# Second-layer memory keys and values projected between the sparse attention's queries and its items, and kept in DRAM

## The chip, the core and the metric

The kernel runs on one core of a Trainium2 chip. The metric is the device time of one execution in microseconds (us); lower is better. PE is TensorE (matrix products), DVE is VectorE, ACT is ScalarE, POOL is GpSimd, and SP is SyncE, whose in-order queue issues nearly all DMAs here.

## What is computed

Two decoder layers over 512 tokens of width 1024. Layer 0 mixes tokens with latent attention, layer 1 with a sparse attention: an indexer scores keys, the best 128 keys of each query stay, and 16 heads in 4 groups attend to them. After the mixer, each layer attends to 256 memory tokens with 4 heads, and then applies an FFN. The part that the change touches is the memory attention of the second layer:

```
def memory_cross_attention(x, mem, w_q, w_kv, w_o):
    q = (x @ w_q).reshape(b, s, XA_HEADS, XA_HEAD_DIM)
    kv = (mem @ w_kv).reshape(b, m, 2, XA_HEADS, XA_HEAD_DIM)
    k, v = kv[:, :, 0], kv[:, :, 1]
    logits = jnp.einsum('bshd,bmhd->bhsm', q, k).astype(jnp.float32) * (XA_HEAD_DIM ** -0.5)
    p = jax.nn.softmax(logits, axis=-1).astype(v.dtype)
    o = jnp.einsum('bhsm,bmhd->bshd', p, v)
    return o.reshape(b, s, D_MODEL) @ w_o
```

`k` and `v` depend on the memory tokens alone, not on the layer's own state. The top-k selection is `lax.top_k(score, topk)` for each block of 128 queries.

## The kernel before

**Number format.** Every fp32 operand is split into a high and a low half (`split`, L94: ACT casts the high half, L95; DVE or, where `eng` is given, POOL subtracts to get the low half, L96). A product is three matmuls (`mm3`, L115 to L118). A weight chunk (`chunk`, L103) is a 512 KB load into a tile `raw` (3 buffers), split into `wh` and `wl` (5 buffers each). PSUM has banks under the tags "a" and "b"; working tiles are `t` (the small ones of 512 columns, or the large ones of 4x512, of which there are 9).

**Order.** Each engine runs its instructions in a fixed order, which a scheduler settles when the program is built; it follows the order in which the code is written unless something later could go earlier. An instruction that waits holds up all that stands behind it on its engine, and a DMA on SP that waits for its buffer holds up the DMAs behind it.

**The stretch around the change.** In the second layer, after the indexer, DVE runs the top-k rounds (`topk`, L948): 16 rounds for each of three query blocks, each a MAX8 (L953) and a MATCH_REPLACE8 (L954) over 256, 384 or 512 columns, and after a block's last round one TENSOR_SCALAR (L958) that turns the scores into a mask. The rounds are dealt out in the code: 2 before each of 2 key projections, 5 (`NTK`) before each of the 8 query projections `w_q`, 1 (`NTI`) after each item. A query projection is 24 matmuls of 512 columns; its result leaves PSUM through `stack_q_pool` (L891 to L897): one copy and two casts on ACT, two subtractions of 64x512 on POOL.

Then come 16 items (4 query blocks by 4 groups), each with scores (`dsa_scores`, L996; 12 matmuls), a softmax whose row maximum is taken on DVE (L399) and whose exponential is on ACT (L405), transposes (L1020, L1022) and the product with the values (L1032, L1033). The bias tile of each item is loaded from `scr` on SP. The output projection `dsa_o` follows with a LayerNorm for each of four token tiles (L295 to L334).

**Memory attention** (`cross`, L703). The keys and values of head 0 are projected just before it (`xa_kv`, L684: 96 matmuls of 256 columns; the weight halves by ACT and DVE). For each head `hd` the code writes scores, then the query projection of head `hd+1` (48 matmuls of 512 columns), then keys and values of head `hd+1`, then `pv`: 8 transposes (L735), two splits and 12 matmuls. The memory tokens themselves (`load_mem`, L672) are two `raw` tiles, loaded on SP right behind the last `w_q` chunk and split at the start of the cross stage.

Of the kernel before, what the change touches and what calls it, by code (L numbers as in the profile page):

```python
# [11 lines left out]
F32 = mybir.dt.float32  # L12
FR = mybir.dt.float32r
I32 = mybir.dt.int32
AF = mybir.ActivationFunctionType
ALU = mybir.AluOpType
# [4 lines left out]
P = 128  # L21
# [3 lines left out]
NK = D // P  # L25
# [41 lines left out]
def tile_hybrid_mla_dsa_deepnorm_block(ctx: ExitStack, tc: tile.TileContext, A: dict, out: bass.AP):  # L67
# [79 lines left out]
    scr = dp.tile([5, 16, P, GW], F32, name="scr")  # L147
    vscr = dp.tile([16, GW], F32, name="vscr")
    flag = cp.tile([1, 1], I32, name="flag")
    ones = cp.tile([P, 1], F32, name="ones")  # L150
# [520 lines left out]

    def load_mem():  # L672
        m = []
        for c in range(2):
            raw = wp.tile([P, 4, 256], F32, tag="raw", name=nm("raw"), bufs=3)
            nc.sync.dma_start(raw, A["memT"][c])
            for i in range(2):
                h, l = t2(FR, (P, 2, 256)), t2(FR, (P, 2, 256))
                split(h, l, raw[:, 2 * i:2 * i + 2])
                m += [(h[:, 0], l[:, 0]), (h[:, 1], l[:, 1])]  # L680
        return m

    def xa_kv(i, hd, m):
        pk = bank("a", (P, 2, 256))  # L684
        for dt in range(2):
            wh, wl = chunk(A["xa_k"][i, 2 * hd + dt], (P, NK, P))
            for k in range(NK):
                mm3(pk[:, dt], (wh[:, k], wl[:, k]), m[k], k == 0, k == NK - 1)
        Kt = (t2(FR, (P, 2, 256)), t2(FR, (P, 2, 256)))
        split(Kt[0], Kt[1], pk)  # L690
        ws = [chunk(A["xa_v"][i, hd, c], (P, 4, 256)) for c in range(2)]
        pv = bank("a", (P, 2, 256))
# [6 lines left out]
        split(Vt[0], Vt[1], pv)  # L699
        return Kt, Vt  # L700

    def cross(i, XT, m, kv0):
        OT = []  # L703
        kvs = {0: kv0}

# [43 lines left out]
        for hd in range(4):  # L749
            Ss = scores(hd, Q)  # L750
            if hd < 3:
                Q = q_proj(hd + 1)
                kvs[hd + 1] = xa_kv(i, hd + 1, m)
            pv(hd, Ss)
# [120 lines left out]
    out_proj(lambda k: OTs[k], lambda n, c: A["mla_o"][n, c], 4, norm, True)  # L875
    kv0 = xa_kv(0, 0, mem)
    OT = cross(0, norm.XT, mem, kv0)
    norm = Norm(load_ln(0, 1))
# [6 lines left out]
    def stack_q(ps, QA, QB):  # L885
# [3 lines left out]
        nc.vector.tensor_tensor(QB[0:64], ps[64:128], QB[64:128].bitcast(F32), op=ALU.subtract)  # L889

    def stack_q_pool(ps, QA, QB):  # L891
        f = t2()
        nc.scalar.copy(f, ps)
        nc.scalar.copy(QA[0:64], ps[0:64])
        nc.scalar.copy(QB[64:128], ps[64:128])
        nc.gpsimd.tensor_tensor(QA[64:128], f[0:64], QA[0:64].bitcast(F32), op=ALU.subtract)
        nc.gpsimd.tensor_tensor(QB[0:64], f[64:128], QB[64:128].bitcast(F32), op=ALU.subtract)  # L897

# [62 lines left out]
    todo = [(qt, [i]) for qt in range(1, NT) for i in range(TOPK // 8)]  # L961
    NTK, NTI = 5, 1
    KA, KB = [], []
# [16 lines left out]
    for j in range(8):  # L980
# [7 lines left out]
        else:  # L988
            qa, qb = t2(FR), t2(FR)
        stack_q_pool(pq, qa, qb)  # L990
        Q += [qa, qb]

    OTd = [(t2(FR), t2(FR)) for _ in range(NK)]
# [70 lines left out]
    for i in range(16):  # L1064
        a = 1 if i < LA else 0
        if i != LA:
            run_s(i + 1 + a)
            run_t(i + a)
        dsa_pv(*items[i], *PT.pop(i))
        for _ in range(NTI):  # L1070
            if todo:
                topk(*todo.pop(0))

    load_x(xsp)
    mem = load_mem()
    norm = Norm(load_ln(1, 0))
    out_proj(lambda k: OTd[k], lambda n, c: A["dsa_o"][n, c], 4, norm, True)
    kv0 = xa_kv(1, 0, mem)
    OT = cross(1, norm.XT, mem, kv0)
    norm = Norm(load_ln(1, 1))  # L1080
# [85 lines left out]
```

## Time and profile before

| what | value |
|---|---|
| median of 3 runs (lowest to highest) | 1563.23 us (1559.45 to 1563.29) |
| time of the profiled execution | 1561.3 us |
| span of the profiled execution | 1559.5 us |
| PE busy | 1513.7 us, 97% of the span |
| DVE busy | 998.4 us, 64% |
| ACT busy | 659.1 us, 42% |
| POOL busy | 306.8 us, 20% |
| mean granted PE clock | 0.994 of full speed |

Outside the span lie 1.8 us of the profiled execution. Starts in the rows below are microseconds from the start of the span. A busy PE is not PE at its peak; a stretch in which PE is idle, or its clock is low, is where time can be won.

### The profile page before, as it was taken

The page shows a single profiled execution, that of the slowest core. Times are in us where ns is not written, and L with a number is a line of the kernel's source. Part 1 is how long each engine was busy: PE and PEld are TensorE (multiplying, and loading weights), DVE is VectorE, ACT ScalarE, POOL GpSimd, SP SyncE. Part 2 cuts the span into 40 slices and gives each one's busy share as a digit, 9 for nine tenths or more (in the row PEclk, how much of TensorE's full clock was granted, in tenths as well). Part 3 has the DMA queues.
Part 4 walks back from the last instruction along what each step waited for, and adds up shares of the span by engine and source line. Part 5 has one row for each costly group of instructions (what it writes and reads, how often), then busy time and mean ns, then how long its engine had stood idle before and what let it go on. Part 6 is the DMA issues. An engine that isn't in the chain of part 4 may idle for free.

```text
span 1559.5 us, 20796 instructions
## 1 busy us (share of the span) xinstructions
PE 1513.7 (97%) x7948; PEld 1290.8 (83%) x7948; DVE 998.4 (64%) x1706; ACT 659.1 (42%) x1182; POOL 306.8 (20%) x303
## 2 busy tenths in 40 slices
PE   8999999999999999999999789999999999999997
PEld 7788778988888888888788678889888888888886
DVE  5887868454746565654668968785448466556545
ACT  4676753343233333332246489434332333333230
POOL 1322101000132331400125522010001323324002
PEclk9999999999999999999999899999999999999999
DMA  6234323322323232223241236243223132322221
GB/s 219 71 103 115 131 87 122 124 93 95 122 96 107 79 120 90 100 88 110 80 149 68 88 122 236 72 143 111 95 95 134 70 122 72 118 95 95 95 95 54
DMA packets 51320, 166.79 MB, mean 107 GB/s; under 512 B 5300, under 2 KB 11748, under 8 KB 49172
## 3 DMA queue, kind: packets, MB, share of 16 engines
q1 hardware_dynamic: 50788, 164.41, 30.8%
q8 instruction: 62, 1.02, 0.3%
q10 hardware_dynamic: 432, 1.05, 0.2%
q14 instruction: 38, 0.31, 0.1%
HBM read 161.20 MB, written 9.47 MB: 109 GB/s over the span
## 4 chain that ended last, share of the span: by engine, by line
PE 78%; DMA 8%; DVE 7%; ACT 4%; issue 1%; POOL 1%; SPq 0%; POOLq 0%; ACTq 0%; DVEq 0%
PE ps L118 24%; PE ps L116 24%; PE ps L117 24%; DMA scr<-vscr 4%; DVE t L96 2%; DVE wl L96 1%; ACT wh L95 1%; DMA raw<-in_mla_o_dram 1%; ACT t L95 1%; ACT t L405 1%; PE ps L324 1%; DVE t L954 1%; POOL sm L267 1%; PE ps L1022 1%; DVE m L953 1%
## 5 line engine op out<-in xcount | busy, mean ns | idle before, releaser
L116 PE MATMUL ps<-t,wh 128*128 128x512 f32 (+1 forms) x1264 | 459.1, 363 | 3.5 <-DVE t L96 3.4
L117 PE MATMUL ps<-t,wh 128*128 128x512 f32 (+1 forms) x1264 | 458.2, 362 | 0.9 <-DVE t L96 0.9
L118 PE MATMUL ps<-t,wl 128*128 128x512 f32 (+1 forms) x1264 | 458.1, 362 | 0.0
L95 ACT CAST wh<-raw 128x1024 fp32r<-128x1024 f32 (+2 forms) x218 | 227.4, 1044 | 470.5 <-PE ps L117 163.3
L96 DVE TENSOR_TENSOR wl<-raw,wh 128x1024 fp32r<-128x1024 f32 (+2 forms) x202 | 260.9, 1293 | 227.7 <-ACT wh L95 225.9
L116 PE MATMUL ps<-wh,t 128*128 128x512 f32 (+2 forms) x838 | 304.9, 364 | 3.8 <-DVE t L96 1.5
L118 PE MATMUL ps<-wh,t 128*128 128x512 f32 (+2 forms) x838 | 303.1, 362 | 1.0 <-DVE t L96 1.0
L117 PE MATMUL ps<-wl,t 128*128 128x512 f32 (+2 forms) x838 | 302.0, 360 | 0.0
L116 PEld LDWEIGHTS ps<-t,wh 128*128 128x128 f32 x1264 | 238.6, 189 | 41.6 <-DVE t L96 5.2
L117 PEld LDWEIGHTS ps<-t,wh 128*128 128x128 f32 x1264 | 238.6, 189 | 37.9 <-DVE t L96 1.4
L118 PEld LDWEIGHTS ps<-t,wl 128*128 128x128 f32 x1264 | 238.6, 189 | 36.7
L116 PEld LDWEIGHTS ps<-wh,t 128*128 128x128 f32 x838 | 158.8, 189 | 27.5 <-ACT t L95 1.8
L118 PEld LDWEIGHTS ps<-wh,t 128*128 128x128 f32 x838 | 158.8, 190 | 24.7 <-DVE t L96 1.4
L117 PEld LDWEIGHTS ps<-wl,t 128*128 128x128 f32 x838 | 158.9, 190 | 23.0
L95 ACT CAST t<-ps 128x512 fp32r<-128x512 f32 (+2 forms) x241 | 118.5, 523 | 132.2 <-PE ps L324 87.6
L265 POOL TENSOR_SCALAR sm<-sm 128x1 f32<-128x1 f32 x32 | 19.5, 608 | 678.9 <-DVE sm L299 635.9
L96 DVE TENSOR_TENSOR t<-ps,t 128x512 fp32r<-128x512 f32 (+2 forms) x241 | 138.7, 603 | 20.4 <-ACT t L95 19.6
L95 ACT CAST wh<-t 128x1024 fp32r<-128x1024 f32 x56 | 58.9, 1052 | 141.6 <-PE ps L117 123.6
L96 DVE TENSOR_TENSOR wl<-t,wh 128x1024 fp32r<-128x1024 f32 x56 | 71.2, 1272 | 64.9 <-ACT wh L95 63.1
L832 DVE TENSOR_TENSOR t<-ps,t 128x512 f32<-128x512 f32 x44 | 30.4, 691 | 120.4 <-PE ps L118 120.4
L96 DVE TENSOR_TENSOR t<-t,t 128x512 fp32r<-128x512 f32 (+2 forms) x113 | 84.0, 746 | 24.3 <-ACT t L95 22.1
L95 ACT CAST t<-t 128x512 fp32r<-128x512 f32 (+3 forms) x137 | 70.5, 525 | 59.6 <-POOL t L766 33.5
(176 smaller groups left out, 1687.5 us busy)
## 6 DMA issues: line engine op xcount, KB each, us to landing
raw<-in_ffn_in_dram SPq DMA_DIRECT2D x88, 512.0 KB, 3.2
t<-in_ffn_dg_dram SPq DMA_DIRECT2D x16, 1024.0 KB, 5.0
raw<-in_xa_k_dram SPq DMA_DIRECT2D x16, 512.0 KB, 3.3
raw<-in_xa_v_dram SPq DMA_DIRECT2D x16, 512.0 KB, 3.8
raw<-in_xa_q_dram SPq DMA_DIRECT2D x16, 512.0 KB, 3.9
raw<-in_xa_o_dram SPq DMA_DIRECT2D x16, 512.0 KB, 3.2
raw<-in_ffn_dl_dram SPq DMA_DIRECT2D x12, 512.0 KB, 3.2
scr<-vscr SPq DMA_DIRECT2D x16, 319.5 KB, 4.2
```

What stands on the lines that cost most here:

```text
L95: nc.scalar.copy(h, src)
L96: (eng or nc.vector).tensor_tensor(l, src, h.bitcast(F32), op=ALU.subtract)
L116: nc.tensor.matmul(ps, st[0], mv[0], start=start, stop=False, skip_group_check=more)
L117: nc.tensor.matmul(ps, st[0], mv[1], start=False, stop=False, skip_group_check=more)
L118: nc.tensor.matmul(ps, st[1], mv[0], start=False, stop=stop, skip_group_check=more)
L265: nc.gpsimd.tensor_scalar(a, var, scale, eps, op0=ALU.mult, op1=ALU.add)
L267: nc.gpsimd.tensor_tensor(b, a, mhalf, op=ALU.pow)
L324: nc.tensor.transpose(pt[:, k], x_of(tt)[:, 512 * n + P * k:512 * n + P * k + P], ident)
L405: nc.scalar.activation(Sx, src, AF.Exp, bias=nb, scale=scale, accum_out=self.sm[:, i:i + 1])
L832: nc.vector.tensor_tensor(sg, pu, sg, op=ALU.mult)
L953: nc.vector.max(out=m8, in_=acc[:, :n])
L954: nc.vector.match_replace(out=acc[:, :n], in_to_replace=m8, in_values=acc[:, :n], imm_value=-3e38)
```

## The change

The keys and values of the second layer are projected after the eight query projections and before the items. `xa_kv` is cut into `xa_k` and `xa_v`; of their 16 weight chunks and of the memory tokens, POOL takes the low halves. The 20 top-k rounds that are left after three before each `w_q` are dealt out over the eight parts, as 3, 3, 3, 3, 2, 2, 2, 2; none stand beside the items. Each part's result (high and low half, 256 KB each) is stored to a DRAM tile `kvd`, 16 stores on SP. In the cross stage `kv_load` reads them back, four loads of 256 KB for each head. The query results leave PSUM through `stack_q` on ACT and DVE. Layer 0 is written in another way but does the same.

```diff
+    kvd = dp.tile([4, 4, P, 512], F32, name="kvd")
...
-    def load_mem():
+    def load_mem(eng=None):
...
-                split(h, l, raw[:, 2 * i:2 * i + 2])
+                split(h, l, raw[:, 2 * i:2 * i + 2], eng)
...
-    def xa_kv(i, hd, m):
+    def xa_k(i, hd, m, eng=None):
...
+        return Kt
+
+    def xa_v(i, hd, m, eng=None):
+        ws = [chunk(A["xa_v"][i, hd, c], (P, 4, 256), eng) for c in range(2)]
...
-                kvs[hd + 1] = xa_kv(i, hd + 1, m)
+                kvs[hd + 1] = kv_of(hd + 1)
...
-    def stack_q_pool(ps, QA, QB):
-        f = t2()
-        nc.scalar.copy(f, ps)
-        nc.scalar.copy(QA[0:64], ps[0:64])
-        nc.scalar.copy(QB[64:128], ps[64:128])
-        nc.gpsimd.tensor_tensor(QA[64:128], f[0:64], QA[0:64].bitcast(F32), op=ALU.subtract)
-        nc.gpsimd.tensor_tensor(QB[0:64], f[64:128], QB[64:128].bitcast(F32), op=ALU.subtract)
...
-    NTK, NTI = 5, 1
+    NTK = 3
...
-        stack_q_pool(pq, qa, qb)
+        stack_q(pq, qa, qb)
         Q += [qa, qb]
+
+    mem = load_mem(nc.gpsimd)
+    for hd in range(4):
+        for j, part in enumerate((xa_k, xa_v)):
+            for _ in range(-(-len(todo) // (8 - 2 * hd - j))):
+                topk(*todo.pop(0))
+            for e, t_ in enumerate(part(1, hd, mem, nc.gpsimd)):
+                nc.sync.dma_start(kvd[hd, 2 * j + e], t_.bitcast(F32).rearrange("p a b -> p (a b)"))
+
+    def kv_load(hd):
+        res = []
+        for j in range(2):
+            ts = (t2(FR, (P, 2, 256)), t2(FR, (P, 2, 256)))
+            for e, t_ in enumerate(ts):
+                nc.sync.dma_start(t_.bitcast(F32).rearrange("p a b -> p (a b)"), kvd[hd, 2 * j + e])
+            res.append(ts)
+        return res
...
-        for _ in range(NTI):
-            if todo:
-                topk(*todo.pop(0))
...
-    mem = load_mem()
...
-    kv0 = xa_kv(1, 0, mem)
-    OT = cross(1, norm.XT, mem, kv0)
+    OT = cross(1, norm.XT, kv_load)
```

Three places show what moves. The first is SP's queue behind the last `w_q` chunk. Before:

```order
L106 DMA raw_11343<-in_w_q_dram 128x1024
L676 DMA raw_12603<-in_memT_dram 128x1024
L676 DMA raw_12613<-in_memT_dram 128x1024
L106 DMA raw_12634<-in_dsa_o_dram 128x1024
L106 DMA raw_12664<-in_dsa_o_dram 128x1024
L106 DMA raw_12694<-in_dsa_o_dram 128x1024
L106 DMA raw_12724<-in_dsa_o_dram 128x1024
L1001 ISA
L1001 DMA t_1657_11398<-scr 128x4x128
```

The same place on SP after the change:

```order
L106 DMA raw_11281<-in_w_q_dram 128x1024
L677 DMA raw_11318<-in_memT_dram 128x1024
L677 DMA raw_11328<-in_memT_dram 128x1024
L106 DMA raw_11348<-in_xa_k_dram 128x1024
L106 DMA raw_11378<-in_xa_k_dram 128x1024
L106 DMA raw_11424<-in_xa_v_dram 128x1024
L106 DMA raw_11430<-in_xa_v_dram 128x1024
L106 DMA raw_11501<-in_xa_k_dram 128x1024
L1014 ISA
L1014 DMA t_1735_11952<-scr 128x4x128
```

The two memory tiles stand where they stood, and hold two of the three `raw` buffers; five chunks of keys and values instead of four of `dsa_o` follow, then the first item's bias.

The second place is ACT behind the last query projections (L893 to L895, or L890 and L891, take a query result out of PSUM; `raw_11318` and `raw_11328` are the memory tokens). Before:

```order
L95 CAST wh_12726<-raw_12724 128x1024
L893 COPY t_1640_11376<-ps_11349 128x512
L894 CAST t_1638_11374<-ps_11349 64x512
L895 CAST t_1639_11375<-ps_11349 64x512
L405 ACT_TABLE_LOAD
L405 ACTIVATE t_1657_11398,sm_11401<-t_1657_11398,sm_11400 128x128 x4
```

On ACT after the change:

```order
L95 CAST wh_11503<-raw_11501 128x1024
L890 CAST t_1615_11312<-ps_11287 64x512
L891 CAST t_1616_11313<-ps_11287 64x512
L95 CAST t_1618_11320<-raw_11318 128x512
L406 ACT_TABLE_LOAD
L406 ACTIVATE t_1735_11952,sm_11955<-t_1735_11952,sm_11954 128x128
L95 CAST t_1620_11324<-raw_11318 128x512
L406 ACTIVATE t_1735_11952,sm_11955<-t_1735_11952,sm_11954 128x128
L95 CAST t_1623_11330<-raw_11328 128x512
```

The memory tokens are now cast here, behind the fifth weight chunk of keys and values and the last query.

The third place is PE at the end of a query projection in the cross stage. Before, where the keys and values of the next head end and `pv` begins (L735 transposes; `t,t` of 128x256 are the next head's scores, of 128x512 the product with the values):

```order
L118 MATMUL ps_13433<-wh_13429,t_2000_12620 128x256
L735 MATMUL ps_13492<-ident,t_2092_13242 128x128 x2
L735 MATMUL ps_13492<-ident,t_2093_13243 128x128 x2
L735 MATMUL ps_13501<-ident,t_2092_13242 128x128 x2
L735 MATMUL ps_13501<-ident,t_2093_13243 128x128 x2
L116 MATMUL ps_13536<-t_2119_13417,t_2108_13348 128x256
L117 MATMUL ps_13536<-t_2120_13418,t_2108_13348 128x256
L118 MATMUL ps_13536<-t_2119_13417,t_2109_13349 128x256
```

On PE after the change, where the query projection of the next head ends:

```order
L118 MATMUL ps_13698<-t_2068_13149,wl_13694 128x512
L739 MATMUL ps_13769<-ident,t_2142_13641 128x128 x2
L739 MATMUL ps_13769<-ident,t_2143_13642 128x128 x2
L739 MATMUL ps_13778<-ident,t_2142_13641 128x128 x2
L739 MATMUL ps_13778<-ident,t_2143_13642 128x128 x2
L116 MATMUL ps_13813<-t_2162_13755,t_2158_13747 128x256
L116 MATMUL ps_13823<-t_2162_13755,t_2158_13747 128x256
L116 MATMUL ps_13787<-t_2168_13774,t_2128_13519 128x512
L116 MATMUL ps_13798<-t_2168_13774,t_2128_13519 128x512
L117 MATMUL ps_13787<-t_2169_13775,t_2128_13519 128x512
```

Between the query projection and the transposes there were 96 matmuls of keys and values; now there are none, and only two score matmuls stand ahead of the product with the values.

## Rows read from the trace of the kernel before

**Rows 1.** The page, part 4: what the chain of waits consists of, by engine.

```profile
PE 78%; DMA 8%; DVE 7%; ACT 4%; issue 1%; POOL 1%; SPq 0%; POOLq 0%; ACTq 0%; DVEq 0%
```

**Rows 2.** Windows (stretch: length, busy us of each engine, PE clock, DMA share).

```profile
885.00:890.00 5.00, 0.84 (x8) 0.64 (x6) 4.86 (x10) 4.26 (x8) 3.39 (x3) 0.87 0.32 104
890.00:895.00 5.00, 0.61 (x3) 0.61 (x3) 4.80 (x13) 4.15 (x6) 4.77 (x4) 0.50 0.55 160
895.00:900.00 5.00, 5.00 (x27) 4.75 (x27) 4.37 (x23) 3.60 (x17) 3.12 (x4) 0.60 0.00 0
900.00:925.00 25.00, 21.58 (x142) 18.08 (x141) 19.31 (x76) 21.06 (x67) 5.00 (x10) 1.00 0.43 138
925.00:950.00 25.00, 23.06 (x139) 19.25 (x140) 15.03 (x48) 21.93 (x59) 5.33 (x13) 1.00 0.40 126
950.00:990.00 40.00, 39.90 (x225) 32.42 (x224) 35.31 (x93) 32.91 (x87) 6.63 (x16) 1.00 0.51 185
```

**Rows 3.** PE's timeline, last query matmul to first item (start, us, instruction, [idle before]).

```profile
884.02 0.39 PE L118 MATMUL ps<-t,wl 128*128 128x512 f32 x1
...
885.56 0.28 PE L1008 MATMUL ps<-t,t 128*128 128x256 f32 x1
894.39 0.58 PE L1006 MATMUL ps<-t,identr 128*128 128x256 f32 x1 [8.55 <-DVE sm L399]
```

**Rows 4.** DVE's timeline during the query projections.

```profile
838.35 0.68 DVE L975 TENSOR_TENSOR t<-ps,t 64x512 fp32r<-64x512 f32 x1
...
854.55 2.35 DVE L958 TENSOR_SCALAR t<-t 128x256 fp32r<-128x256 f32 x1
...
869.79 1.90 DVE L96 TENSOR_TENSOR wl<-raw,wh 128x1024 fp32r<-128x1024 f32 x1
...
875.44 0.54 DVE L954 MATCH_REPLACE8 t<-m,t 128x384 f32<-128x384 f32 x1
...
894.03 0.29 DVE L399 CUSTOM_DVE_ANT_0 t<-ps,t 128x128 f32<-128x128 f32 x1
```

**Rows 5.** ACT's timeline: casts of two `dsa_o` chunks, and what they waited for.

```profile
884.25 1.05 ACT L95 CAST wh<-raw 128x1024 fp32r<-128x1024 f32 x1 [6.49 <-DMA raw<-in_dsa_o_dram]
...
890.78 1.04 ACT L95 CAST wh<-raw 128x1024 fp32r<-128x1024 f32 x1 [1.38 <-DMA raw<-in_dsa_o_dram]
```

**Rows 6.** POOL's timeline: a weight split and subtractions of query results.

```profile
859.57 2.41 POOL L96 TENSOR_TENSOR wl<-raw,wh 128x1024 fp32r<-128x1024 f32 x1
...
869.32 1.29 POOL L896 TENSOR_TENSOR t<-t,t 64x512 fp32r<-64x512 f32 x1 [7.35 <-issue]
870.69 2.15 POOL L897 TENSOR_TENSOR t<-t,t 64x512 fp32r<-64x512 f32 x1
```

**Rows 7.** DMA issues from 840 to 960 us (count, KB each, median us to landing).

```profile
raw<-in_dsa_o_dram SPq DMA_DIRECT2D x6, 512.0 KB, 3.8
...
t<-scr SPq DMA_DIRECT2D x4, 256.0 KB, 3.9
raw<-in_w_q_dram SPq DMA_DIRECT2D x1, 512.0 KB, 3.3
```

**Rows 8.** PE's timeline: LayerNorm transposes (L324), head 0's keys and values between.

```profile
1031.36 1.04 PE L324 MATMUL ps<-ident,t 128*128 128x128 f32 x8
...
1032.35 0.28 PE L117 MATMUL ps<-t,wh 128*128 128x256 f32 x1
...
1037.98 0.28 PE L116 MATMUL ps<-wh,t 128*128 128x256 f32 x1
...
1041.30 0.63 PE L324 MATMUL ps<-ident,t 128*128 128x128 f32 x4 [1.36 <-DVE t L320]
```

**Rows 9.** Timelines of ACT and of DVE in the cross stage.

```profile
1078.43 0.58 ACT L95 CAST t<-ps 128x512 fp32r<-128x512 f32 x1
...
1078.56 1.23 DVE L96 TENSOR_TENSOR wl<-raw,wh 128x1024 fp32r<-128x1024 f32 x1 [1.66 <-ACT wh L95]
1079.70 0.69 DVE L96 TENSOR_TENSOR t<-ps,t 128x512 fp32r<-128x512 f32 x1
```

More of the change, by code (lines that the diff above doesn't have):

```diff
@@ L678, in load_mem @@
                 h, l = t2(FR, (P, 2, 256)), t2(FR, (P, 2, 256))
-                split(h, l, raw[:, 2 * i:2 * i + 2])
+                split(h, l, raw[:, 2 * i:2 * i + 2], eng)
                 m += [(h[:, 0], l[:, 0]), (h[:, 1], l[:, 1])]
         return m
-    def xa_kv(i, hd, m):
+    def xa_k(i, hd, m, eng=None):
         pk = bank("a", (P, 2, 256))
         for dt in range(2):
-            wh, wl = chunk(A["xa_k"][i, 2 * hd + dt], (P, NK, P))
+            wh, wl = chunk(A["xa_k"][i, 2 * hd + dt], (P, NK, P), eng)
             for k in range(NK):
@@ L690, in xa_kv @@
         split(Kt[0], Kt[1], pk)
-        ws = [chunk(A["xa_v"][i, hd, c], (P, 4, 256)) for c in range(2)]
+        return Kt
+    def xa_v(i, hd, m, eng=None):
+        ws = [chunk(A["xa_v"][i, hd, c], (P, 4, 256), eng) for c in range(2)]
         pv = bank("a", (P, 2, 256))
@@ L699, in xa_kv, with cross @@
         split(Vt[0], Vt[1], pv)
-        return Kt, Vt
-    def cross(i, XT, m, kv0):
+        return Vt
+    def cross(i, XT, kv_of):
         OT = []
-        kvs = {0: kv0}
+        kvs = {0: kv_of(0)}
         def q_proj(hd):
@@ L875, in tile_hybrid_mla_dsa_deepnorm_block @@
     out_proj(lambda k: OTs[k], lambda n, c: A["mla_o"][n, c], 4, norm, True)
-    kv0 = xa_kv(0, 0, mem)
-    OT = cross(0, norm.XT, mem, kv0)
+    kv0 = xa_k(0, 0, mem), xa_v(0, 0, mem)
+    OT = cross(0, norm.XT, lambda hd: (xa_k(0, hd, mem), xa_v(0, hd, mem)) if hd else kv0)
     norm = Norm(load_ln(0, 1))
```

## The prediction

> **What bounds the kernel now.** I read the chain of waits first: PE's own work is 78% of it, and DMA, DVE and ACT hold most of the rest [rows 1]. The change adds no matmul and takes none away, so it can win only where PE stands idle or runs at a low clock, and lose only where it opens new holes. So I went to the windows next. Around the place to which the work moves they show one bad stretch [rows 2]: PE is busy 0.84 of 5 us from 885 us, 0.61 of the next 5, and the clock, which is 1.00 elsewhere, is granted at 0.50 and then 0.60 until 900. From 900 to 950 it is idle 25 - 21.58 + 25 - 23.06 = 5.4 us, and from 950 on PE is full (39.90 of 40). PE's timeline gives the hole its cause [rows 3]: 8.55 us of idle time until DVE has taken the first item's row maxima (L399), and DVE does that at 894.03, after the top-k rounds and weight splits queued ahead of it [rows 4]. The drop to the 1.2 GHz level comes with that idle time. Twenty-seven matmuls at about half speed between 895 and 900 cost about 2.3 us. So 8.55 + 2.3 + 5.4 = 16.3 us is all that can be had here.
>
> **Unit costs.** A matmul of 256 columns in a stream takes 0.1198 us: 47 of them lie between 1032.35 and 1037.98 [rows 8]. The moved work is 4 heads x 96 = 384 matmuls, 46.0 us, away from the cross stage and into the new place. A query projection is 24 matmuls x 0.227 = 5.44 us; the eighth ends at 884.25 [rows 3]. A weight split costs 1.05 us on ACT [rows 5], and 2.41 us on POOL [rows 6] against 1.23 on DVE [rows 9]. A 512 KB chunk lands 3.3 to 3.8 us after its issue [rows 7].
>
> **Part 1: the query projections.** `stack_q` puts two subtractions of 0.68 us [rows 4] per projection into DVE's queue between the top-k rounds, where POOL did them beside it. Projection 6 needs the bank of projection 4, whose subtractions stand behind the fifteenth round of 384 columns. Before, that round ends at 875.44 + 0.54 = 876.0 [rows 4]; the change puts four subtractions ahead of it (+2.6) and takes one weight split out (1.90 minus its overlap, -1.7). The mask instruction, 2.35 us there, took that long beside a POOL split that will now stand elsewhere, so up to 1.9 us more may go. With the two subtractions (1.3) the bank comes free between 876.3 and 878.2. Unhindered, projection 6 would start at 884.25 - 2 x 5.44 = 873.4. I take the early end, +3.0, and 0.9 for projection 7, which waits in the same way behind projection 5: the queries end at 888.2, and item 0's scores (1.5 us) at 889.7. ACT loses its eight copies here; that is worth nothing, since ACT waits in this stretch for DMAs [rows 5].
>
> **Part 2: when keys and values can start.** The two memory tiles take two of the three `raw` buffers as before, so the weight chunks go one after another through one buffer; before, it is the `dsa_o` chunks that do so, 6.5 us from one to the next [rows 5]. Now one turn is 3.3 load + 1.05 ACT + 2.41 POOL = 6.8 us. The buffer comes free when the last `w_q` chunk is split, at 859.57 + 2.41 = 862.0 [rows 6], or up to 1.5 us earlier, as POOL no longer has subtractions in front. The fifth chunk then lands at 860.5 + 4 x 6.8 + 3.3 = 891.0, or 892.5. ACT casts the memory tokens only behind that chunk's cast (1.05) and the last query's two (1.2), and POOL subtracts behind that chunk's split: the first memory half is ready around 895.5 and the last around 900. So PE is idle from 889.7 to about 895.5, the clock falls as it did in the hole of [rows 2], and by 902 some 37 matmuls are done. The other 347 x 0.1198 = 41.6 us end at 943.7. Chunks for them come every 2.4 us (POOL) against 24 x 0.12 = 2.9 us of matmuls, so they keep up. The items begin at 943.7 instead of 894.4: +49.3, or **+3.3 us** beyond the moved 46.0. The bounds are -4.7 (no hole at all: 889.7 + 46.0 = 935.7 against 894.4 + 46.0) and +8 (late ends of both chains).
>
> Row 870.69 shows a POOL subtraction at 2.15 us instead of 1.29, beside DVE's split of 1.90 us [rows 4, 6]. The Trainium skill (GPSIMD Reference, Specifications) says that POOL shares its SBUF interfaces with VectorE and contends with instructions that read two SBUF inputs, which agrees. By that rule alone, four POOL splits that each met such an instruction would put the start back by 4 x 0.9 = 3.4 us as an estimate; but the 2.41 us split ran beside top-k rounds [rows 6], and rounds are what stands there now.
>
> **Part 3: the items.** They lose the top-k rounds, the `dsa_o` loads in front of their bias loads, and the cold start. Of the 2.3 + 5.4 = 7.7 us in [rows 2], ACT's exponentials remain a limit (21.06 and 21.93 of 25 us). I take **-5**, between -8 and -2.
>
> **Part 4: the cross stage.** Keys and values were also its filler. At its start they run from 1032.15 until the last LayerNorm tile comes out; the transposes start at 1041.30 with 1.36 us idle [rows 8]. Now only the first half of head 0's queries is ready, 48 x 0.12 = 5.8 us, to 1037.9: idle 3.4 us, **+2.0** (0 to 3.5). At three head boundaries the transposes follow the query projection directly. If that ends at t, ACT has a `xa_o` cast (1.05, waiting for the projection's weight buffer), then the last query half (0.58) and the two transposed tiles [rows 5, 9]: their high halves come at t+2.1 and t+2.7. DVE follows with a split of 1.23 and three of 0.69 [rows 9]: the low halves come at t+3.6 and t+4.2. PE has 0.8 us of transposes, 0.24 of scores and 0.45 of `pv` until then, and idles about 2 us: three times, **+6** (0 to 8, less if buffers order ACT otherwise). No row shows a reload of 256 KB from DRAM written by the kernel; the nearest are 3.9 us for 256 KB of bias and 3.3 for 512 KB [rows 7]. For heads 1 to 3 the loads stand on SP behind `xa_o` chunks that wait for a DVE split at about t-3, and the scores ask for them at t+0.8: **0** (0 to +3). Stores hide beside the matmuls, since the DMA share here is 0.3 to 0.55 [rows 2].
>
> The Trainium skill (DMA: Bandwidth & Descriptors, Anatomy of one DMA) gives a fixed 2.0 us plus bytes over 436 GB/s; as an estimate that is 2.6 us for 256 KB, and the reload would then be hidden. No row has this kind of load.
>
> **The sum.** 3.3 - 5 + 2 + 6 = +6.3 us on the profiled execution's 1561.3 (span 1559.5 and 1.8 around it): 1567.6. That execution lies 1.9 us under the median of 1563.23, inside the spread of the runs. I say **1568**.
>
> **Rivals.** (1) *The hole is filled.* If memory tokens and first chunks are split by the time the queries end, Part 2 gives -4.7 instead of +3.3, Part 3 -6, and the boundaries half: -4.7 - 6 + 2 + 3 = -6, about 1555. For it: DVE's queue, which made the 8.55 us, is no longer in PE's way. Against it: the single `raw` buffer, whose pace [rows 5] shows. (2) *A wash.* The boundaries hide, because the schedule's margins there are a microsecond: 3.3 - 5 + 2 = 0, about 1562. (3) *Slower still, by late reloads.* The loads wait on SP behind `xa_o`; if they land at t+3 or later instead of t+0.8, each boundary loses 2 us more, and the head-0 loads, which wait for buffers that the items hold, may add 3: +6.3 + 9 = +15, about 1577. It decides once a landing takes more than 4 us; the longest row near it says 3.9 [rows 7]. The work itself surely moves: the orders show it.
>
> **How the numbers follow.** Chances: 0.45 for the sum as forecast (+2 to +11), 0.22 for rival 1, 0.21 for rival 2, 0.12 for rival 3. A measurement can tell about 0.3%, 4.7 us. Of the forecast case a third lies below that (0.13), the rest above. Faster 0.22; same 0.21 + 0.13 = 0.34; slower 0.32 + 0.12 = 0.44. All low ends together would be -4.7 - 8 = -12.7, all high ends +20; neither is likely at once, so the range goes from 1552 to 1578, which holds most of rival 1 and of rival 3. The forecast case alone is 1563 to 1573.
>
> **What would show it.** Right: the eighth query projection ends near 888; PE then idles 4 to 6 us until the memory splits, with a clock window near 0.5; keys and values end near 944; the holes and the low clock in the items' windows shrink from 7.7 us to about 3; and the cross stage has three holes of 2 us, behind DVE splits. Wrong: a full PE from 884 to 936, or reloads named as what PE waited for, or cross-stage windows that are as full as before.

## The result, and the profile after

The changed kernel takes 1571.06 us, median of 6 runs (1567.86 to 1572.53); the kernel before took 1561.02 us in the same comparison, median of 6 (1558.69 to 1563.29). The ratio is 1.0062, with a 95% interval from 1.0049 to 1.0075: slower by about 0.6%, 10 us. The forecast was 1568, in a range from 1552 to 1578. The profiled execution has a span of 1570.4 us against 1559.5.

The page first, parts 1 and 4 (busy time of PE; the chain of waits by engine):

```profile
PE 1522.9 (97%) x7948; PEld 1296.0 (83%) x7948; DVE 988.1 (63%) x1702; ACT 655.5 (42%) x1174; POOL 328.9 (21%) x307
...
PE 77%; DMA 8%; DVE 6%; ACT 4%; issue 2%; POOL 2%; SPq 0%; POOLq 0%; ACTq 0%; DVEq 0%
```

Beside [rows 1], PE's share of the chain fell from 78 to 77% and DVE's from 7 to 6, while `issue` and POOL went from 1 to 2. The same 7948 matmuls are there. So little is to be seen in the whole, and the stages have to be taken apart. The table cuts both traces at four places on PE: the last matmul of the indexer's scores (832.77 us before, 833.88 after; the same 226 matmuls of the key and query projections follow it), the first matmul of the items that stands behind the queries (before) or behind the moved work (after), the LayerNorm transposes of [rows 8] (1031.36 before, 1077.95 after), and the last of these transposes. The 1.1 us by which the first mark differs lie ahead of everything that was changed; over the profiles of this study that mark, behind the same instructions, stands between 829.6 and 835.2, so times of two runs are compared from that mark on. The second mark does not part quite the same matmuls: of the scores of the first two items, 12 stand ahead of it before and 18 after, so 6 x 0.12 = 0.7 us of the first two differences have only moved from one row to the next (+3.0 and -3.5 without them).

| stretch, us | before | after | difference | without the 46.0 moved |
|---|---|---|---|---|
| projections to items | 61.62 | 111.34 | +49.72 | +3.7 |
| items to LayerNorm transposes | 136.97 | 132.73 | -4.24 | -4.2 |
| first to last such transposes | 9.94 | 9.78 | -0.16 | with the next row |
| last transposes to the end | 518.2 | 482.67 | -35.5 | +10.3 for both |
| sum | 726.7 | 736.5 | | +9.8 |

The first stretch in windows (stretch: length, then busy us of PE, weight loads, DVE, ACT and POOL, PE's granted clock, DMA share, GB/s), to be held against [rows 2]:

```profile
835.00:885.00 50.00, 46.90 (x200) 38.38 (x199) 47.66 (x123) 20.11 (x28) 20.45 (x11) 0.97 0.24 84
885.00:890.00 5.00, 5.00 (x23) 4.14 (x23) 4.81 (x10) 4.07 (x7) 2.40 (x1) 1.00 0.03 10
890.00:895.00 5.00, 2.53 (x17) 1.99 (x15) 4.29 (x10) 2.81 (x5) 1.27 (x1) 0.96 0.82 262
895.00:900.00 5.00, 3.84 (x16) 3.55 (x17) 4.91 (x18) 4.97 (x14) 4.45 (x4) 0.50 0.27 105
900.00:905.00 5.00, 5.00 (x38) 5.00 (x38) 4.83 (x11) 1.23 (x4) 1.64 (x2) 0.85 0.60 210
905.00:950.00 45.00, 45.00 (x374) 44.74 (x373) 20.66 (x42) 22.74 (x37) 28.11 (x13) 1.00 0.77 264
950.00:975.00 25.00, 21.92 (x148) 18.63 (x145) 12.20 (x57) 20.84 (x69) 5.26 (x14) 1.00 0.44 144
975.00:990.00 15.00, 13.81 (x84) 11.57 (x85) 8.35 (x29) 13.74 (x35) 2.49 (x6) 1.00 0.39 129
```

And the waits in it, from PE's timeline (start, us, instruction, idle before and what ended it):

```profile
877.73 0.76 PE L116 MATMUL ps<-t,wh 128*128 128x512 f32 x1 [3.10 <-DVE t L893]
...
894.22 0.39 PE L1019 MATMUL ps<-t,identr 128*128 128x256 f32 x1 [2.37 <-DVE sm L400]
...
895.54 0.58 PE L116 MATMUL ps<-t,wh 128*128 128x256 f32 x1 [0.64 <-ACT t L95]
...
897.38 0.58 PE L117 MATMUL ps<-t,wh 128*128 128x256 f32 x1 [0.62 <-POOL t L96]
```

The 8.55 us hole of [rows 3] is gone; in its place stand 3.10 us at the seventh query projection, behind DVE's subtractions (L893), then 2.37 us at the second item's scores and some 1.3 us at the memory tokens. The clock falls all the same: the window from 895 to 900 is granted 0.50 of the full clock, the 1.2 GHz level, as 890 to 895 was in [rows 2]. From 905 to 950 PE is full. It is DVE's maxima (L400) and the memory splits that now end late, where the top-k rounds ended late before. Both hang on the weight chunks, as the timelines of ACT, of DVE and of SP's queue show:

```profile
885.81 1.05 ACT L95 CAST wh<-raw 128x1024 fp32r<-128x1024 f32 x1 [4.77 <-DMA raw<-in_xa_v_dram]
...
892.61 1.04 ACT L95 CAST wh<-raw 128x1024 fp32r<-128x1024 f32 x1 [2.13 <-DMA raw<-in_xa_k_dram]
...
894.87 0.62 ACT L95 CAST t<-raw 128x512 fp32r<-128x512 f32 x1
...
893.87 0.29 DVE L400 CUSTOM_DVE_ANT_0 t<-ps,t 128x128 f32<-128x128 f32 x1 [0.54 <-DMA t<-scr]
...
889.37 0.33 SPq L106 DMA_DIRECT2D raw<-in_xa_k_dram  x1
889.99 1.69 SPq L1014 DMA_DIRECT2D t<-scr  x3
```

The chunks are cast 6.8 us apart (885.81 and 892.61), the memory tokens only behind the fifth of them (894.87); and the first item's bias, the last thing that its maxima wait for, is issued on SP right behind that fifth chunk (889.99 behind 889.37).

In the cross stage the LayerNorm hole and the three head boundaries of the prediction are there. PE's timeline at the LayerNorm, and at the first two boundaries:

```profile
1087.73 1.23 PE L325 MATMUL ps<-ident,t 128*128 128x128 f32 x8 [3.00 <-DVE t L321]
...
1110.37 1.03 PE L739 MATMUL ps<-ident,t 128*128 128x128 f32 x8
1111.94 1.01 PE L116 MATMUL ps<-t,t 128*128 128x256 f32 x3 [0.55 <-ACT t L95]
1113.34 0.49 PE L116 MATMUL ps<-t,t 128*128 128x512 f32 x1 [0.38 <-DVE t L96]
...
1131.23 0.47 PE L116 MATMUL ps<-t,t 128*128 128x256 f32 x2 [0.32 <-DMA t<-kvd]
```

The transposes (L739) start at 1110.37, 1129.87, 1150.97 and 1162.04, so a head takes 19.5, then 21.1 us. In windows, around the LayerNorm and the second boundary:

```profile
1085.00:1090.00 5.00, 2.19 (x12) 1.71 (x13) 4.23 (x7) 1.18 (x2) 0.00 (x0) 0.92 0.51 190
1090.00:1095.00 5.00, 5.00 (x33) 4.90 (x32) 0.31 (x1) 0.81 (x1) 0.00 (x0) 0.74 0.00 0
...
1130.00:1135.00 5.00, 3.93 (x17) 2.62 (x16) 3.02 (x4) 2.39 (x4) 0.00 (x0) 0.86 0.79 268
1135.00:1140.00 5.00, 5.00 (x29) 4.45 (x29) 2.39 (x7) 1.42 (x3) 0.00 (x0) 0.80 0.00 0
```

Both holes cost more than their idle time, as the clock is granted at 0.74 to 0.86 behind them. The reloads' side is SP's queue, and the view of the tile `kvd`:

```profile
1096.53 11.31 SPq L106 DMA_DIRECT2D raw<-in_xa_o_dram  x3
1107.92 1.82 SPq L1002 DMA_DIRECT2D t<-kvd  x4
1112.71 14.41 SPq L106 DMA_DIRECT2D raw<-in_xa_o_dram  x2
1127.17 1.85 SPq L1002 DMA_DIRECT2D t<-kvd  x4
...
  PE ps L116: 0.6, 2
...
DMA to landing us min/median/max: 3.9/4.8/5.0
```

A head's four reloads are issued 2.4 to 2.7 us ahead of the transposes, behind `xa_o` chunks for which the queue stood 11 to 16 us, and take 3.9 to 5.0 us to land. PE waits for them by name twice, 0.6 us in all. Whether they cost only that is what the experiments had to tell.

### The profile page after: what moved, and what is told of

It reads as the page before. It is cut to its first block, busy times and chain, and to the rows that moved or that the text cites. A ratio compares the mean times of both kernels' runs of the same rounds, so it can differ in the third digit from the quotient of the medians.

```text
span 1570.4 us, 20875 instructions
## 1 busy us (share of the span) xinstructions
PE 1522.9 (97%) x7948; PEld 1296.0 (83%) x7948; DVE 988.1 (63%) x1702; ACT 655.5 (42%) x1174; POOL 328.9 (21%) x307
## 4 chain that ended last, share of the span: by engine, by line
PE 77%; DMA 8%; DVE 6%; ACT 4%; issue 2%; POOL 2%; SPq 0%; POOLq 0%; ACTq 0%; DVEq 0%
PE ps L118 24%; PE ps L117 24%; PE ps L116 24%; DMA scr<-vscr 4%; DVE t L96 2%; ACT wh L95 1%; DVE wl L96 1%; POOL wl L96 1%; ACT t L95 1%; DMA t<-scr 1%; POOL sm L268 1%; PE ps L325 1%; ACT t L406 1%; DMA raw<-in_xa_k_dram 1%; DVE t L321 1%
## 5 line engine op out<-in xcount | busy, mean ns | idle before, releaser
L96 DVE TENSOR_TENSOR wl<-raw,wh 128x1024 fp32r<-128x1024 f32 (+2 forms) x186 | 241.0, 1297 | 214.3 <-ACT wh L95 212.7
L96 POOL TENSOR_TENSOR wl<-raw,wh 128x1024 fp32r<-128x1024 f32 x32 | 76.9, 2406 | 107.4 <-ACT wh L95 98.6
```

What stands on the lines that cost most here:

```text
L96: (eng or nc.vector).tensor_tensor(l, src, h.bitcast(F32), op=ALU.subtract)
```

## The experiments

Two questions stood behind the result. In the cross stage, +10.3 us: is the boundary loss the chain through ACT and DVE that the prediction names, or the late reload? And at the start, +3.7 us: is it the single weight buffer, which holds up the memory tokens, and can the items use an earlier end? All ratios are to the kernel before, taken on the same chip in the same comparison; the changed kernel stands at 1.0062.

**No reload between heads.** One reload, of head 0, serves all four heads, so the other heads' keys and values are not those of the reference; the amount of PE's work is the same.

```diff
-    OT = cross(1, norm.XT, kv_load)
+    kv0 = kv_load(0)
+    OT = cross(1, norm.XT, lambda hd: kv0)
```

> The changed kernel, but the cross stage reads head 0's keys and values back once and uses them for all four heads (12 of the 16 loads are left out, and the output differs by that). Theory (the loss of the cross stage is the chain of ACT casts and DVE subtractions behind each query projection, about 2.2 us at a head boundary): the period from head to head stays within 0.5 us of the 19.5 and 21.1 us of the changed kernel, and the time within 1.5 us of it, so a ratio near 1.006 to the kernel before. Rival (the reloads from DRAM arrive late): the waits on the reloaded tiles go, about 1.5 to 3 us at each of three boundaries, 4 to 9 us in all, so a ratio of 1.000 to 1.003.

Measured: 1564.96 us, ratio 1.0017 (1.0007 to 1.0027). PE's timeline and windows of this run:

```profile
1087.94 1.23 PE L325 MATMUL ps<-ident,t 128*128 128x128 f32 x8 [3.01 <-DVE t L321]
...
1109.06 1.03 PE L739 MATMUL ps<-ident,t 128*128 128x128 f32 x8
1126.83 1.04 PE L739 MATMUL ps<-ident,t 128*128 128x128 f32 x8
...
1085.00:1090.00 5.00, 1.98 (x12) 1.40 (x13) 4.24 (x7) 1.17 (x2) 0.00 (x0) 1.00 0.59 202
1090.00:1095.00 5.00, 5.00 (x43) 5.00 (x43) 1.54 (x2) 1.53 (x2) 0.00 (x0) 1.00 0.00 0
```

Both full heads take 17.8 us (1109.06 to 1126.83 to 1144.59), and the wait behind the transposes is gone, although ACT and DVE have the same casts and splits to do. The chain alone doesn't make the holes. What changed is also the order on PE: here most of the next head's scores stand between the transposes and `pv` and cover the chain; in the changed kernel all but two of them stand behind `pv` (from 1116.33 on). Nothing but the loads differs between the two kernels, so it is the reload that moved the scores back, already when the program's order was settled. My theory fell, the rival held.

**Queries in halves around the transposes.** The transposes are put between the two halves of the next head's query projection, so that half a projection covers the chain.

```diff
+            if hd < 3 and i == 1:
+                q0 = q_half(hd + 1, 0)
+                kvs[hd + 1] = kv_of(hd + 1)
+                PT = pv_t(Ss)
+                Q = [q0, q_half(hd + 1, 1)]
+                pv_mm(hd, PT)
+                continue
```

> The changed kernel, but in the second layer the transposes of a head's probabilities stand between the two halves of the next head's query projection, and the product with the values behind the second half. Theory (uncovered ACT and DVE chain): 5.4 us of matmuls now cover the chain of the transposed tiles, and 2.7 us of products cover that of the last query half; three boundaries of about 2.2 us shrink to under 0.4 us each, and the low clock at 1133 to 1136 us (1.6 us) goes: 5 to 8 us faster than the changed kernel, ratio 1.001 to 1.003. Rival (late reloads): the scores still wait for their keys, at most 2 us faster.

Measured: 1564.91 us, 1.0009 (0.9999 to 1.002); heads of 17.4 us, and no wait for `kvd` in the view of that tile. It mends both causes at once, since the reloads are asked for earlier too, so it can't tell them apart; it shows that what stands at the boundaries is worth some 8 us.

**The reload a head earlier.** Everything is computed and loaded as in the changed kernel, only the loads are written ahead of the scores of the head before.

```diff
+            if hd < 3 and i == 1:
+                kvs[hd + 1] = kv_of(hd + 1)
             Ss = scores(hd, Q)
```

> The changed kernel, but each head's reload is written ahead of the scores of the head before, so that its four loads are issued a whole head earlier; all work is kept. Theory (the keys come back late: the loads are issued 2.3 us before the scores ask and land 3.9 to 5.0 us later, and the order settled at build time therefore puts the scores behind the product with the values): as with the single reload, the head period goes to about 17.8 us and the time to a ratio of 1.001 to 1.003. Rival (the 12 loads themselves cost time, by DMA traffic or buffers): the gain of the single reload is not reached, ratio 1.004 to 1.006.

Measured: 1563.53 us, 1.0017 (1.0008 to 1.0026), the same as with no reload at all. SP's queue and the view of `kvd` (landing):

```profile
1093.74 1.85 SPq L1006 DMA_DIRECT2D t<-kvd  x4
...
DMA to landing us min/median/max: 3.9/4.9/6.2
```

The loads take as long as before, but are issued 13 us ahead of the transposes (1107.18), and the heads take 17.8 us. Most of the next head's scores again stand ahead of `pv`, as in the run without reloads. So the boundary loss is the reload's lateness, with the order that it brings; no run parts the wait from the order.

**POOL's subtractions back.** `stack_q_pool` takes the place of `stack_q` again, the rest as changed.

```diff
-        stack_q(pq, qa, qb)
+        stack_q_pool(pq, qa, qb)
```

> The changed kernel with the query results taken out of PSUM as in the kernel before (ACT copies, POOL subtractions). Theory (the start of keys and values is set by the chain of weight chunks through one raw buffer and the memory tokens behind it): the 3.1 us wait and the slow clock in the query projections go, and these end about 5 us earlier, near 885, but keys and values still start between 894 and 900, since POOL's subtractions now stand in that chain too: time within 2 us of the changed kernel, or up to 3 us slower. Rival (the query wait is what delays keys and values): 4 to 5 us faster than the changed kernel, ratio near 1.003.

Measured: 1579.97 us, 1.0117 (1.0099 to 1.0135), 8.6 us slower than the changed kernel by the ratios, which neither the theory (3 us at most) nor the rival foresaw. PE's timeline:

```profile
894.32 0.58 PE L1027 MATMUL ps<-t,identr 128*128 128x256 f32 x1 [5.74 <-DVE sm L400]
```

Another 6.07 us at 904.14 wait for a POOL split of the memory tokens, and the items begin 120.46 us behind the first mark instead of 111.34. DVE's two subtractions per projection are thus the cheaper place by 9 us as soon as POOL has the weight splits of the moved work.

**Memory tokens ahead of the queries.** They are loaded and split before the query projections.

```diff
+    mem = load_mem(nc.gpsimd)
     Q = []
...
-    mem = load_mem(nc.gpsimd)
     for hd in range(4):
```

> The changed kernel with the memory tokens loaded and split ahead of the query projections, which leaves three raw buffers for the weight chunks of keys and values. Theory (chain through one raw buffer): keys and values start as soon as the queries and the first scores end, near 892 instead of 895.5, with no hole of 2.4 us and no half clock behind it; they end near 938 instead of 945: 5 to 8 us faster than the changed kernel, ratio 1.001 to 1.003, with the 3.1 us wait in the query projections still there. Rival (top-k rounds on DVE, or the first item's bias, set the start): less than 2 us faster.

Measured: 1569.68 us, 1.004 (1.0027 to 1.0052), by the ratios 3.4 us better than the changed kernel, between the two forecasts. Keys and values start at 891.35, 58.3 us behind the first mark instead of 61.7, and PE is full from 885 to 937, so the cause named for the start is right; the items begin at 104.40 instead of 111.34, 6.9 us earlier. Of this, 2.2 us are 18 score matmuls of the first items, which stood ahead of the items' mark and now stand behind it. The items then take 139.43 us, 6.7 more than in the changed kernel: these 2.2, 2.4 of idle PE time (7.8 against 5.4) and 1.7 of a low clock, granted at 0.91 and 0.92 in the two windows from 950 to 970. In this profile the stretch gave nearly all of it back.

**The same, and small tiles for two more query results.** Queries 2 and 3 are put into small tiles instead of a large one, which frees a large tile for the items' biases.

```diff
-        if j < 4:
+        if j < 2:
             if j % 2 == 0:
                 qt8 = t8()
```

> The run with the memory tokens split early, and besides the query results 2 and 3 go into four small tiles instead of one of the nine large ones, so that no projection's bank waits for a large tile and DVE's subtractions stand evenly between the top-k rounds. Theory: the wait of 3 to 4 us in the query projections and the low clock behind it go, the queries end at 884 to 885 as before, keys and values at about 932; since a large tile is free earlier, the first bias loads come earlier too, so the gain is kept through the items: 4 to 8 us faster than with the early memory tokens alone, ratio 0.997 to 1.001. Rival (the items are held by their bias loads behind the dsa_o chunks on SP, wherever keys and values end): less than 2 us faster, ratio 1.003.

Measured: 1563.18 us, 1.0015 (1.0006 to 1.0024), 4 us better than the run before, the low end of the theory. No wait is left on PE from 870 to 900; the items begin at 97.74 and take 140.29, against 111.34 and 132.73. Without the 2.2 us of score matmuls, 11.4 us are won at the start against the changed kernel, and 5.4 are given back. Here the trace says where: PE's, ACT's and DVE's timelines at the first item, and the windows.

```profile
940.00 0.58 PE L1019 MATMUL ps<-t,identr 128*128 128x256 f32 x1 [5.46 <-DVE sm L400]
...
936.84 1.04 ACT L95 CAST wh<-raw 128x1024 fp32r<-128x1024 f32 x1 [0.98 <-DMA raw<-in_dsa_o_dram]
...
939.05 0.68 DVE L96 TENSOR_TENSOR t<-ps,t 128x512 fp32r<-128x512 f32 x1
939.66 0.28 DVE L400 CUSTOM_DVE_ANT_0 t<-ps,t 128x128 f32<-128x128 f32 x1
...
935.00:940.00 5.00, 0.00 (x0) 0.00 (x1) 3.91 (x7) 4.00 (x6) 0.00 (x0) 0.76 0.86 275
940.00:945.00 5.00, 5.00 (x26) 5.00 (x26) 3.40 (x20) 3.91 (x17) 0.40 (x1) 0.56 0.72 255
```

The first item's maxima (L400) stand on DVE behind the splits of the last keys and values and of `dsa_o` chunks; those wait for ACT's casts, and ACT for chunks that are still landing. In the changed kernel the same item's scores run ahead of keys and values, at 890, and the work of 45 us covers its softmax; here, as in the run before, keys and values are ready when the queries end, and the built order puts the scores behind them, at 932.94, with nothing to cover them. The hole of 5.46 us and some 20 matmuls at a pitch of 0.21 instead of 0.12 us (1.9 us) make 7.4 us; the items' other holes are 2.0 us smaller than in the changed kernel (3.4 against 5.4), which leaves the 5.4.

**`dsa_o` chunks on POOL's queue.** The run before, with these loads off SP's queue, where the items' bias loads stand behind them.

```diff
-        nc.sync.dma_start(raw[:, :n], src)
+        (q or nc.sync).dma_start(raw[:, :n], src)
...
-    out_proj(lambda k: OTd[k], lambda n, c: A["dsa_o"][n, c], 4, norm, True)
+    out_proj(lambda k: OTd[k], lambda n, c: A["dsa_o"][n, c], 4, norm, True, nc.gpsimd)
```

> The run with early memory tokens and small query tiles, with the eight dsa_o chunk loads issued on POOL's queue instead of SP's. Theory (the items' bias loads stand on SP behind dsa_o chunks that wait for a buffer, which is why the items give back what an earlier end of keys and values wins): the bias loads begin before 938 instead of 945, and the stretch from the start of the items to the last dsa_o tile goes from 140 us to 133 to 136: 3 to 7 us faster, ratio 0.997 to 1.000. Rival (the items are held by ACT's exponentials or by the large tiles, not by SP's queue): within 1.5 us, ratio 1.001 to 1.002.

Measured: 1562.27 us, 1.0012 (1.0003 to 1.0021), not to be told from the run without it. SP's queue and PE's timeline:

```profile
940.01 52.94 SPq L1014 DMA_DIRECT2D t<-scr  x12
...
934.03 0.58 PE L1019 MATMUL ps<-t,identr 128*128 128x256 f32 x1 [3.90 <-DVE sm L400]
```

The twelve bias loads begin 5.5 us earlier (940.01 against 945.54), but so does all of this execution: its first mark lies at 829.85 instead of 835.20, and from there the loads begin at 110.2 against 110.3 us. They take as long, 53 us, in which SP waits for the items' matmuls (L1033 27.8 us, L1035 11.6, L1021 10.2) to give tiles free; the items take 139.0 instead of 140.3 us. So the `dsa_o` chunks on SP's queue were not what the bias loads waited for. The hole behind L400 is still there, 3.90 us.

**Small tiles alone**, without the early memory tokens (the `if j < 2` edit on the changed kernel).

> The changed kernel with query results 2 and 3 in small tiles and nothing else: the 3.1 us wait in the query projections is taken away alone, the memory tokens stay late. Theory (the two delays lie one behind the other only at their start; the chain of weight chunks through one raw buffer sets the start of keys and values by itself): queries end near 885 on the old scale, but keys and values still start at 894 to 896, 60 to 62 us after the start of the key projections: at most 1.5 us faster than the changed kernel, ratio 1.005 to 1.006. Rival (the query wait delays the start): 3 to 5 us faster, ratio 1.003.

Measured: 1566.28 us, 1.0036 (1.0022 to 1.0049), 4 us better than the changed kernel: the rival's figure, not the theory's. Its profile speaks for the theory. The queries do end earlier, and PE then waits:

```profile
891.76 0.58 PE L1019 MATMUL ps<-t,identr 128*128 128x256 f32 x1 [6.87 <-DVE sm L400]
```

Keys and values start 61.6 us behind the first mark, against 61.7 in the changed kernel, and the items begin at 111.18. But that profiled execution took 1570.8 us, the other four 1564.6 to 1566.3. So the profile shows one execution in which early queries were worth nothing while the memory tokens came late; where the other four won their 4 us is open.

**Head 0's keys and values left in the cross stage**, as cover for the LayerNorm hole; three heads are moved.

```diff
-    for hd in range(4):
+    for hd in range(1, 4):
...
+    mem = load_mem()
     norm = Norm(load_ln(1, 0))
...
-    OT = cross(1, norm.XT, kv_load)
+    kv0 = xa_k(1, 0, mem), xa_v(1, 0, mem)
+    OT = cross(1, norm.XT, lambda hd: kv_load(hd) if hd else kv0)
```

> The changed kernel, but head 0's keys and values (96 of the 384 matmuls) stay at the start of the cross stage, as in the kernel before, with the memory tokens loaded and split a second time there. Theory (these matmuls cover the last LayerNorm tile): the 3.0 us hole at 1087 us shrinks to 1.4 us or less, no low clock behind it; 2 to 5 us faster than the changed kernel, ratio 1.003 to 1.005. Rival (the loss of the cross stage lies at the head boundaries alone): within 1 us of the changed kernel, ratio 1.006.

Measured: 1573.31 us, 1.0086 (1.0072 to 1.0101), where a gain was expected. The cross stage did get better: with 34.5 us moved, the two last stretches lose 5.1 us beyond them instead of 10.3. But the items take 143.55 us instead of 132.73. PE's timeline and SP's queue:

```profile
936.06 0.58 PE L1019 MATMUL ps<-t,identr 128*128 128x256 f32 x1 [4.79 <-DVE sm L400]
...
918.48 0.33 SPq L677 DMA_DIRECT2D raw<-in_memT_dram  x1
...
973.40 23.15 SPq L1014 DMA_DIRECT2D t<-scr  x6
```

The memory tokens' second load needs two of three `raw` buffers among the items, the last six bias loads begin only at 973.40, and an item's maxima lie uncovered again (the wait stands in the third item's scores). The expectation looked at the cross stage alone.

**Combinations.** First all of: memory tokens early, small tiles, head 0 late, reloads a head earlier.

> All of it: memory tokens early, query results 2 and 3 in small tiles, head 0's keys and values at the start of the cross stage, the reload of heads 1 to 3 a head earlier. Theory: the gains add, about 5 to 8 us at the start, 3 in front of the cross stage, 5 to 7 at the head boundaries: 14 to 18 us faster than the changed kernel, and so faster than the kernel before, ratio 0.994 to 0.998. Rival (the items take back what the start gains): ratio 0.998 to 1.001.

Measured: 1558.7 us, 0.9987 (0.9977 to 0.9996), as the rival has it. The stretch behind the last LayerNorm transposes is 483.7 us, exactly 518.2 - 34.5: nothing is lost there. The items take 146.70 us, with 8.25 us of idle time behind L400. Then memory tokens early, small tiles, early reloads and queries in halves, with all four heads moved:

> Memory tokens early, query results 2 and 3 in small tiles, the reload a head earlier, and the transposes between the halves of the next query projection; all four heads' keys and values stay in the new place. Theory: 7 us as in the run with the first two, and 7 to 8 us in the cross stage as in the run with the split: about 15 us faster than the changed kernel, ratio 0.995 to 0.998. Rival (the gains share one cause and do not add): ratio 1.000 to 1.002.

Measured: 1556.19 us, 0.9975 (0.9965 to 0.9984), faster than before. And the same with `dsa_o` on POOL's queue:

> The former two together. Theory: the gains add, ratio 0.991 to 0.995. Rival: no faster than the better of the two.

Measured: 1552.35 us, 0.9951 (0.9937 to 0.9965): the best of the study, 8 us below the kernel before and, by the two ratios, some 17 below the changed one. Moving `dsa_o` made no difference to tell by itself (1.0012 against 1.0015) and makes 3.8 us by the medians here; but the two profiled executions have spans of 1552.5 and 1552.0 us, so no trace shows where these come from. The two longest of PE's waits that are left in it, from the list of waits from 830 to 1130 us (us in total, times, longest):

```profile
PE ps L1039 <- DVE sm L400: 4.5, 1, 4.5
PE ps L325 <- DVE t L321: 2.2, 1, 2.2
```

The first table again, for the runs that tell most (us, with the ratio; LayerNorm's own, 9 to 10 us everywhere, left out; in the last three rows 2.2 us of score matmuls count as items that count under "to items" in the first four):

| kernel | to items | items | last part | ratio |
|---|---|---|---|---|
| changed | 111.34 | 132.73 | 482.67 | 1.0062 |
| one reload for all heads | 110.99 | 134.86 | 474.56 | 1.0017 |
| reload a head earlier | 111.39 | 133.48 | 476.8 | 1.0017 |
| POOL's subtractions back | 120.46 | 133.54 | 482.15 | 1.0117 |
| memory tokens early | 104.40 | 139.43 | 482.1 | 1.0040 |
| the same, small tiles | 97.74 | 140.29 | 480.1 | 1.0015 |
| all of it, `dsa_o` on POOL | 99.16 | 138.58 | 475.6 | 0.9951 |

## Why the prediction was right, and where it was not

**Queries and start of keys and values (parts 1 and 2).** Right in mechanism and size. The seventh projection waited 3.10 us behind DVE's subtractions (forecast +3.0); keys and values began at 895.54 (895.5) and ended at 945.1 (943.7), of which 1.1 us lie ahead of the change: +3.7 beyond the moved work (0.7 of it scores) against +3.3. The chain is the forecast one: the chunks turn in 6.8 us, as forecast, and the memory tokens are cast behind the fifth. That the late tokens set the start is shown from both sides, counted from the first mark: early tokens bring it from 61.7 to 58.3 us, with early queries to 51.5, and early queries alone leave it at 61.6. The last rests on one profiled execution, while the median of that run was 4 us better. Before the start PE idled 3.6 us, not 4 to 6: 2.37 of it stand behind the maxima, which the prediction did not name. The 0.9 us for the eighth projection did not come as a wait; instead the seventh's matmuls ran at a pitch of 0.43 instead of 0.227 us until 880.9, which cost about 1.5 us.

**Items (part 3).** -4.2 (-3.5 without the moved scores) against -5, with one of its two terms. The cold start is gone: the clock is granted at 1.00 over all of the items. The small holes are not: from the second mark to the LayerNorm transposes PE is busy 131.50 of 136.97 us before and 127.33 of 132.73 after, idle 5.5 and 5.4 us, where about 3 were forecast. So taking the top-k rounds and the `dsa_o` loads away from the items shrank no hole. What the prediction did not see is why the cold start went: item 0's softmax is now covered by the moved matmuls, because its scores stand ahead of them. Where the scores stand behind them, an earlier start is given back in part.

**Cross stage (part 4).** +10.3 against +8; this is the term that was mis-sized, and one of its causes was wrong. Run against run: taking the reloads out gives 8.1 us back (482.67 - 474.56). Of these, the head periods hold 19.5 - 17.8 = 1.7, 21.1 - 17.8 = 3.3 and, at the last pair, 11.1 - 9.7 = 1.4, together 6.4, against a forecast of 6; of these, 1.7 is the low clock from 1130 to 1140 (5 x 0.14 + 5 x 0.20), so the holes alone cost 4.7. The rest, 1.7, is the low clock behind the LayerNorm hole (5 x 0.08 + 5 x 0.26), which this run's profile lacks. What remains, 474.56 - (518.2 - 46.0) = 2.4 us, is the LayerNorm hole itself, forecast at 2.0. So the holes cost 4.7 and 2.4 us, against 6 and 2, and the low clock behind two of them, 3.4 us, was left out of the sum, although the first part of the prediction had priced it for the hole of [rows 3].

The step that failed is the boundary's cause. "ACT/DVE chain behind the query projection" is a true chain, and PE does wait for it (1.1 us behind ACT's casts and 1.2 behind DVE's splits at the three boundaries, 0.6 behind the reloads), but it costs next to nothing when the next head's scores are there to run under it: 17.8 us a head, against 17.4 with the queries in halves. They were not, since the reload is late: it was priced at 0 on a landing bound of 3.9 us and an issue at t-3. It is issued at t-2.4 to t-2.7 and lands in 4.8 us, and the built order puts most scores behind `pv`. The point from which rival 3 was to decide, a landing over 4 us, was passed; but the late keys came in place of the chain's price rather than on top of it. The price was worked out on the order that the program has, with the scores behind `pv`, so the size held though the cause of that order was missed; that is luck as much as reckoning. Of the signs of being wrong, one did show, if faintly: PE's waits name the reloads.

The reload is also where the estimate of 2.6 us from the Trainium skill stood. The measured landing is 3.9 to 5.0 us with a median of 4.8, so its figure (the Trainium skill, DMA: Bandwidth & Descriptors, Anatomy of one DMA), which that section fits for DMAs on the gpsimd path, is too small for these loads, which SP issues four in a row; the measurement decides.

**The rivals.** Rival 1 (a filled hole) didn't happen in the changed kernel, and could be made: with early tokens and small tiles PE is full from 870 on. Its price was wrong in two places: without the score matmuls that changed sides, the start gives -8.4 us instead of -4.7, and the items +1.9 instead of -6. Rival 2 (the boundaries hide) is what an earlier reload gives: 1.0017, 7 us better than the changed kernel.

## What to carry to other kernels

When matmuls are moved into a hole, look up what they covered where they stood, and what they will cover where they go: of the 10.3 us that the cross stage lost here, the LayerNorm hole (2.4, and 1.7 for the low clock behind it) is lost cover, and with head 0's keys and values left there, and the reloads a head earlier, nothing is lost. A result kept in DRAM has to be asked for early: 2.4 to 2.7 us ahead was too late here, a head (13 us) ahead was enough. A late load is paid twice, in the wait and in the order that the program takes around it. And a start that comes earlier is worth only what the next chain (here the first item's maxima, behind casts of chunks that are still landing) can use of it.

## What the hardware showed beyond that

Reloads of 256 KB from a tile that the kernel wrote itself took 3.9 to 5.0 us, no less than 512 KB of weights in [rows 7] (3.3 to 3.8). The granted clock did not answer to a hole of the same length in the same way each time: behind the LayerNorm hole of 3.00 us it went to 0.92 and 0.74, behind that of 3.01 us in the run without reloads, and of 3.09 us in the run with `dsa_o` on POOL's queue, it stayed at 1.00. Which of the two a run gets was not settled; it moves the time by some 1.7 us. The `dsa_o` chunks landed later in the changed kernel than before, 5.2 us at the median against 3.8 in [rows 7], and moving them to POOL's queue made no clear difference: from SP 5.2 and 4.4 us, from POOL 4.9 and 5.2, in two pairs of kernels that differ in the queue alone.
